# Two-layer hybrid DiT block: the first layer's middle modulation tiles by TensorE in column groups, and the stacking pattern loaded from DRAM

## The chip, the cores and the metric

The kernel runs on one core of one Trainium2 chip. The metric is the device time of one execution in microseconds. Engines are named as in the profile: PE (TensorE, matrix products), DVE (VectorE), ACT (ScalarE), POOL (GpSimd) and SP (SyncE, which issues most of the DMA transfers); ACT issues DMA transfers as well. Each engine runs its own instructions in order.

## The reference

The model has two layers. A modulation vector per layer comes from the conditioning c (and, for the 256 context tokens, from c_ctx):

```python
silu_c, silu_cc = silu(c), silu(c_ctx)
sh1, sc1, g1, sh2, sc2, g2 = split(silu_c @ ada_w[layer] + ada_b[layer], 6)        # 6 x 1024 columns
csh1, csc1, cg1, csh2, csc2, cg2 = split(silu_cc @ ada_w[layer] + ada_b[layer], 6)
a_l = rms_norm(h, norm1_g) * (1 + sc1) + sh1       # a_c likewise from hc
p = a @ w_in[layer]                                # columns of three head groups
d = diff_mixer(...)    # 4 heads, softmax(q1 k1) - lam * softmax(q2 k2), heads of 32
q = gqa_mixer(...)     # 6 query heads on 2 key heads of 64
n = gdn_mixer(...)     # gated DeltaNet: conv, l2 norm, chunks of 64, triangular solve, both directions
h = h + g1 * (concat(d, q, n) @ w_out)
h = h + g2 * swiglu(modulate(rms_norm(h, norm2_g), sh2, sc2))
```

There are 512 latent and 256 context tokens, and 1024 model columns. Only the latent stream is returned, after a last norm. The modulation has 48 column tiles of 128 per layer (6 x 1024), each for two conditionings. Tiles 0 to 15 (shift and scale of the first norm) are wanted first, tiles 16 to 23 (g1) after the output projection, 24 to 39 (shift and scale of the second norm) before the feed-forward part, 40 to 47 (g2) at the end.

## The kernel before

Activations lie with model columns on partitions. Projection products are split into three fp32r products: a weight block lands in a `raw` buffer, ACT rounds it to `whi`, DVE subtracts to get `wlo`, and PE multiplies ahi by whi, ahi by wlo and alo by whi. The ring `W` has three raw buffers of 128x1024 floats (512 KB); the `adaw` tiles of the modulation take their buffers from the same three. The weight loads that concern us (`w_t`, L160) and the adaw loads (L299) are issued from ACT's queue.

In layer 0 the start-up computes the norm and, in `ada_half` (L321 to L343), the first 16 modulation tiles: fp32 matmuls with the two conditionings (cT) as the weights and ada_w as the moving operand, 512 columns each, in two column groups. Then follow `gdn_inproj` (nine column tiles of the gated DeltaNet projection with their convolutions, PSUM tiles `gps`, evicted by ACT to `conv`), `zab` (six token tiles, PSUM tiles `tps`), and the groups dqk, kv and gq (six token tiles each). Between the groups, as `EARLY` (L41) orders it, stand the preparations ("0" to "5"), inversions ("v0" to "v2", the v0 of layer 0 on DVE, the other two on POOL) and posts of the DeltaNet part. After them the attention region begins, whose order `PLAN` (L37) gives; its start is `pick_setup` (L1080).

The 24 tiles 16 to 39 of layer 0 are made one per token tile of zab, dqk, kv and gq: `tok_group` calls `ada_next`, which loads a 512 KB tile of the transposed ada_w (128 output columns on partitions, 1024 inputs in a row) and, in `ada_row`, forms two row sums, one for each conditioning, against `cb`, that is silu(c) broadcast over the partitions by `ada_rows`. A row sum is one DVE operation with an accumulator (L183, output `junk`); for tiles 20 to 35 the second one is a product on POOL and an accumulating ACT copy. POOL adds the bias into `md`. The other layers' tiles and tiles 40 to 47 are made the same way, later.

`pick` is a 0/1 matrix of 128 x 4 x 128 by which PE stacks q and k heads (matmuls `stk`); `pick_setup` builds it with 64 DVE operations of 32x32 in each layer.

The order of instructions on each engine is set at build time by a scheduler that simulates the engines, from the order of the code and priorities; so a change of code in one place can move instructions of others.

Of the kernel before, what the change touches and what calls it, by code (L numbers as in the profile page):

```python
# [2 lines left out]

# [6 lines left out]
F32 = mybir.dt.float32  # L10
F32R = mybir.dt.float32r
I32 = mybir.dt.int32
AF = mybir.ActivationFunctionType
ALU = mybir.AluOpType
AX = mybir.AxisListType

D = 1024
KT = 8
# [21 lines left out]
INV_DVE = ((0,), (0, 2))  # L40
EARLY = ("0 1 2 5 4 v0 q v1 3 p0 p1 q q v2",  # L41
         "0 1 2 v0 5 v1 3 q p0 4 q p1 v2 q")
ADA_POOL = (tuple(range(20, 36, 1)), ())
LATF = (3, 4)
GORD = (("dqk", "kv", "gq"),) * 2
HORD = ((0, 2, 1, 3, 4),) * 2
# [52 lines left out]
class Net:  # L99
# [197 lines left out]
    def ada_row(self, R, w, l, ct, src, queue):  # L297

        queue.dma_start(out=w, in_=src)  # L299
        m = self.md[l][:, ct]  # L300
        j = R.tiny("junk", [128, 1024], mybir.dt.bfloat16)
        for ci in range(2):
            if ci == 1 and ct in ADA_POOL[l]:
                self.mul(w, w, self.cb[ci], self.g)
                self.act(w, w, AF.Copy, scale=0.5, accum_out=m[:, ci:ci + 1])
            else:
                self.stt(j, w, 0.5, self.cb[ci], ALU.mult, ALU.mult, accum_out=m[:, ci:ci + 1])
        self.add(m, m, self.adab[:, l, ct:ct + 1].to_broadcast([128, 2]), self.g)

    def ada_next(self):  # L310
# [10 lines left out]
    def ada_half(self, i, ws, pt):  # L321


        pd = self.big("adaps", i)
        ps, pd = pd[:, 0], (pd[:, 0], pd[:, 1])
        for kt, w in enumerate(ws):
            if i == 0:
                hi, lo = (self.R.tiny(n, [128, 1024], F32R, bufs=3) for n in ("adahi", "adalo"))
                for s in range(2):
                    j = slice(512 * s, 512 * s + 512)  # L330
                    self.cp(hi[:, j], w[:, j])
                    self.sub(lo[:, j], w[:, j], hi[:, j].bitcast(F32))
                for s in range(2):
                    j = slice(512 * s, 512 * s + 512)
                    self.mm(pd[s][0:4], self.cS[:, kt], hi[:, j], kt == 0, False)
                    self.mm(pd[s][0:4], self.cZ[:, kt], lo[:, j], False, kt == KT - 1)
                continue
            for s in range(2):
                self.lastrow = self.t.matmul(ps[64 * s:64 * s + 2], self.cT[:, kt], w[:, 512 * s:512 * s + 512], start=kt == 0, stop=kt == KT - 1).ins
        row = self.R.tiny("adar", [4, 2, 512], bufs=1)  # L340
        m = 4 if i == 0 else 2
        self.cp(row[0:m, 0], pd[0][0:m])
        self.v.tensor_copy(row[0:m, 1], pd[1][0:m] if i == 0 else ps[64:66])  # L343
        for s in range(2):
            for t in range(4):
                self.t.transpose(pt[:, 16 * s + 4 * t:16 * s + 4 * t + m], row[0:m, s, 128 * t:128 * t + 128], self.ident[0:m, 0:m])
        pv = pt[:, 0:32].rearrange("p (s t c) -> p s t c", s=2, c=4)
        md = self.md[0][:, 0:16].rearrange("p (s h t) c -> p s h t c", s=2, h=2)[:, :, i]
        b = self.adab[:, 0, 0:16].rearrange("p (s h t) -> p s h t", s=2, h=2)[:, :, i]
        self.add(md, pv[:, :, :, 0:2], b.unsqueeze(3).to_broadcast([128, 2, 4, 2]))  # L350
        if i == 0:
            self.add(md, md, pv[:, :, :, 2:4])
        kts = slice(4 * i, 4 * i + 4)
        self.stt(self.A1[0][:, 0, kts], md[:, 1], 1.0, self.gains[:, 0, kts].unsqueeze(2).to_broadcast([128, 4, 2]), ALU.add, ALU.mult)

    def ada_scale(self, l, n):
        o = 8 if n == 0 else 32
# [131 lines left out]
    def gdn_inproj(self, l):  # L489
        self.tokm = [[None] * 3 for _ in range(3)]  # L490
        for kind in range(3):
            for gi in range(3):
                if kind == 0 and gi == 0 and l == DEPTH - 1:
                    continue
                self.tokm[kind][gi] = self.G.slot("tokm", tag="k")
        self.gunits = {}
        if l > 0:
            self.gfirst = {}
        lat, ctx = (CTX, LAT, 262), (0, CTX, 2)
        order = (3, 4, 5, 0, 1, 2, 6, 7, 8)  # L500
        banks = {}
        for half in ((0, 256), (256, 256)):
            for i, ct in enumerate(order[:HALF[l]]):
                if ct not in banks:
                    banks[ct] = (self.mm_bank if i < 2 else self.aux)("gps")
                self.gdn_mm(l, ct, *lat, banks[ct], [half])
        for ct in order[HALF[l]:max(len(self.gfirst), LATF[l])]:
            self.gdn_mm(l, ct, *lat)
        for ct in order:
            if ct not in order[:max(LATF[l], HALF[l], len(self.gfirst))]:  # L510
                self.gdn_mm(l, ct, *lat)
            if ct > 2 or l < DEPTH - 1:
                self.gdn_mm(l, ct, *ctx)
            self.gdn_ct(l, *divmod(ct, 3))

    def tok_group(self, l, name, ncols, tiles, cols=None):
# [5 lines left out]
        for tt in tiles:  # L522
            lo_c, hi_c = cols(tt) if cols else (0, ncols)
            n = hi_c - lo_c
            ps = self.mm_bank("tps")
            for kt in range(KT):
# [4 lines left out]
                self.mm(ps[:, lo_c:hi_c], ah, wh, kt == 0, False)  # L531
                self.mm(ps[:, lo_c:hi_c], ah, wl, False, False)
                self.mm(ps[:, lo_c:hi_c], al, wh, False, kt == KT - 1)
            self.ada_next()
            yield tt, ps

    goff = {"zab": 0, "dqk": 8 * 408, "kv": 8 * 920, "gq": 8 * 1432}
# [542 lines left out]
    def pick_setup(self):  # L1080

        self.pick = self.R.tiny("pick", [128, 4, 128], F32R)
        for r in range(4):
            rows = slice(32 * r, 32 * r + 32)
            for j, at in enumerate(((0, 1), (2, 3), (0, 2), (1, 3))):
                for b in range(4):
                    self.v.tensor_scalar(out=self.pick[rows, j, 32 * b:32 * b + 32], in0=self.ident[rows, rows], scalar1=float(b in at), scalar2=None, op0=ALU.mult)

    def parts_of(self, t0):

# [370 lines left out]
    def build(self):  # L1461
# [7 lines left out]
        for l in range(DEPTH):  # L1469
# [2 lines left out]
            self.G = self.region("gdn%d" % l, sb, SLOT, k=12)  # L1472
            self.GP = self.P1 = self.region("prep%d" % l, sb, SLOT, s=P1S[l])
            self.R = self.region("proj%d" % l, sa, 512, s=PROJS[l])
            self.gdn_inproj(l)
            self.wprio, self.wafter = WPRIO[l], None
            if l == 0:
                self.ada_todo = [(0, ct) for ct in range(16, 40)]
                self.ada_rows(self.R)
            self.zab(l)  # L1480
            self.gdn_begin(l)
            proj = self.attn_proj(l)
# [31 lines left out]
            for kt in range(KT):  # L1514
                x = self.N.slot("h", tag="h")
# [13 lines left out]
            for b, R in self.ffn(l, whole, parts):  # L1529
                if last:  # L1530
                    for kt in range(KT):
                        x = self.hs(kt, *b[:2])
# [26 lines left out]
def shape_consts():  # L1559
    f = np.float32  # L1560
    i = np.arange(128)
    same = (i[:, None] // 64) == (i[None, :] // 64)
    l, j = i[:, None], i[None, :]
# [13 lines left out]
    def rope(rot):  # L1577
# [6 lines left out]
        t = np.stack([cc, ssn], 1).reshape(4, 128, 2, rot)  # L1584
        return np.ascontiguousarray(t.transpose(1, 0, 2, 3))

    return {"ident": np.eye(128, dtype=f), "masks": masks.reshape(128, 768), "mloc": mloc,
            "negm": np.concatenate([negm.reshape(128, 128), masks[:, 2:4].reshape(128, 256)], 1), "blk2": blk2,
            "rope_d": rope(32), "rope_g": rope(64)}

# [1 line left out]
def layout(inp):  # L1592
# [8 lines left out]
    aw = a["ada_w"]  # L1601
    o["ada_t"] = aw.transpose(0, 2, 1).reshape(96, 128, D)
    o["ada_q"] = aw[0, :, :2 * D].reshape(KT, 128, 2, 2, 512).transpose(3, 0, 1, 2, 4).reshape(2, KT, 128, D)
    o["adab"] = a["ada_b"].reshape(DEPTH, 48, 128).transpose(2, 0, 1)
    g = np.concatenate([a["norm1_g"], a["norm2_g"], a["final_norm_g"][None]], 0)
    o["gains"] = g.reshape(5, KT, 128).transpose(2, 0, 1)
    w = a["w_in"]
# [40 lines left out]
```

## Time and profile before

| | us |
|---|---|
| median of 3 runs | 2253.53 (2251.14 to 2255.30) |
| profiled execution | 2248.59 |
| span of the profiled execution, first to last instruction | 2246.8 |
| mean granted clock of PE in it | 0.923 |
| busy in the span: PE, DVE, ACT, POOL | 2019.5, 1466.3, 866.6, 562.8 |

The time of the profiled execution and its span differ by 1.8 us, which lies before the first and after the last instruction. Busy time of an engine is the time in which it had an instruction in work; the rest is waiting, and the view of lines says what ended it. In the trace, times are microseconds from the start of the span; PE is the matmuls and PEld the loads of weights, which may overlap them. "gps<-ahi,whi" means that gps is written from ahi and whi. A bracket behind a row of the timeline is the idle time of that engine before the row, and what ended it.

### The profile page before, as it was taken

The numbers are of one execution on the slowest core, as the hardware profiler recorded it, in microseconds if no ns is written. First come the engines' busy times: TensorE is split into PE (matmuls) and PEld (weight loads), VectorE is DVE, ScalarE is ACT, GpSimd is POOL, SyncE is SP. The second block draws the span as 40 slices with busy tenths as digits, with TensorE's granted clock in tenths as the row PEclk, the third lists the DMA queues.
The fourth block names the chain that finished last, engine by engine and source line by source line (L and its number), as shares of the span: only waits on it lengthen the run. The fifth ranks groups of instructions, "written<-read, shape, count | busy, mean of one in ns | idle before, by whom it ended". The sixth has DMA issues, their size and how long they took to land. (4 is left out here: it accounts for less than half of the span.)

```text
span 2246.8 us, 37406 instructions
## 1 busy us (share of the span) xinstructions
PE 2019.5 (90%) x14588; PEld 1680.6 (75%) x14588; DVE 1466.3 (65%) x2756; ACT 866.6 (39%) x1738; POOL 562.8 (25%) x835
## 2 busy tenths in 40 slices
PE   7997865889889999999999989985799899999997
PEld 3885654666668888888888888764567688888887
DVE  6888896857653766746667467678767745434444
ACT  5443322665662421212121344322466644222223
POOL 2137687522003300000000240347213022000002
PEclk9998975799889999999999989996589999999999
DMA  8145543221033334433334321443312153322331
GB/s 303 53 148 151 166 142 96 47 63 48 25 137 123 100 114 140 142 102 127 128 108 146 107 71 54 131 122 93 68 31 65 38 189 100 97 79 95 104 104 61
DMA packets 167601, 237.01 MB, mean 105 GB/s; under 512 B 75329, under 2 KB 109249, under 8 KB 167425
## 3 DMA queue, kind: packets, MB, share of 16 engines
q10 hardware_dynamic: 46160, 144.92, 19.8%
q1 hardware_dynamic: 121264, 89.70, 13.3%
q8 instruction: 115, 1.88, 0.3%
q14 instruction: 62, 0.50, 0.1%
HBM read 198.53 MB, written 36.04 MB: 104 GB/s over the span
## 5 line engine op out<-in xcount | busy, mean ns | idle before, releaser
L189 ACT ACTIVATE whi<-raw 128x1024 fp32r<-128x1024 f32 (+4 forms) x246 | 220.8, 912 | 470.2 <-PE dps L192 200.6
L165 DVE TENSOR_TENSOR wlo<-raw,whi 128x1024 fp32r<-128x1024 f32 (+4 forms) x236 | 249.2, 1069 | 197.0 <-ACT whi L189 196.2
L192 PE MATMUL gu<-ahi,wlo 128*128 128x512 f32 x672 | 262.5, 391 | 1.6 <-DVE wlo L165 1.6
L192 PE MATMUL gu<-ahi,whi 128*128 128x512 f32 x672 | 262.2, 391 | 0.0
L183 DVE SCALAR_TENSOR_TENSOR junk<-adaw,cb 128x1024 bf16<-128x1024 f32 x144 | 179.7, 1248 | 40.9 <-DMA adaw<-ada_t 39.9
L192 PE MATMUL dps<-acth,whi 128*128 128x512 f32 (+1 forms) x560 | 184.3, 344 | 0.6 <-ACT acth L189 0.4
L192 PE MATMUL dps<-acth,wlo 128*128 128x512 f32 (+1 forms) x560 | 183.9, 344 | 0.0
L192 PE MATMUL gu<-alo,whi 128*128 128x512 f32 x672 | 167.0, 390 | 0.0
L165 POOL TENSOR_TENSOR md<-md,adab 128x2 f32<-128x2 f32 x80 | 44.2, 555 | 451.4 <-DVE junk L183 449.0
L192 PE MATMUL tps<-whi,ahi 128*128 128x512 f32 (+4 forms) x368 | 138.0, 378 | 15.0 <-ACT gk L189 12.5
L183 DVE SCALAR_TENSOR_TENSOR h<-dps,md,h 128x512 f32<-128x512 f32 (+1 forms) x128 | 80.4, 632 | 104.8 <-PE dps L192 104.7
L1140 DVE TENSOR_REDUCE nm<-S 128x1 f32<-128x768 f32 (+1 forms) x140 | 117.3, 844 | 47.9 <-PE S L192 46.9
L192 PEld LDWEIGHTS gu<-ahi,wlo 128*128 128x128 f32 x672 | 126.3, 188 | 28.1 <-DVE wlo L165 2.0
L192 PEld LDWEIGHTS gu<-alo,whi 128*128 128x128 f32 x672 | 126.1, 188 | 26.7
L192 PEld LDWEIGHTS gu<-ahi,whi 128*128 128x128 f32 x672 | 126.3, 188 | 25.7
L165 POOL TENSOR_TENSOR sqc<-sqc 128x256 f32<-128x256 f32 x35 | 34.4, 983 | 435.7 <-ACT sqc L186 435.2
L192 PE MATMUL tps<-wlo,ahi 128*128 128x512 f32 (+4 forms) x368 | 139.0, 378 | 2.5 <-DVE wlo L165 2.5
L192 PE MATMUL tps<-whi,alo 128*128 128x512 f32 (+4 forms) x368 | 137.4, 374 | 0.0
L186 ACT ACTIVATE P<-S,nm 128x768 f32<-128x768 f32 (+1 forms) x140 | 114.3, 817 | 45.3 <-DVE nm L1140 33.0
L192 PE MATMUL dps<-actl,whi 128*128 128x512 f32 (+1 forms) x560 | 122.9, 344 | 0.0
L192 PEld LDWEIGHTS dps<-acth,whi 128*128 128x128 f32 x560 | 105.2, 188 | 15.2 <-ACT acth L189 0.6
L192 PEld LDWEIGHTS dps<-acth,wlo 128*128 128x128 f32 x560 | 105.2, 188 | 14.5
(311 smaller groups left out, 4846.9 us busy)
## 6 DMA issues: line engine op xcount, KB each, us to landing
raw<-w_u ACTq DMA_DIRECT2D x88, 512.0 KB
adaw<-ada_t ACTq DMA_DIRECT2D x80, 512.0 KB
raw<-w_o ACTq DMA_DIRECT2D x24, 512.0 KB
raw<-w_d ACTq DMA_DIRECT2D x44, 256.0 KB
raw<-w_d ACTq DMA_DIRECT2D x32, 320.0 KB
adaq<-ada_q SPq DMA_DIRECT2D x16, 512.0 KB
raw<-w_t ACTq DMA_DIRECT2D x16, 512.0 KB
h<-h SPq DMA_DIRECT2D x16, 384.0 KB
```

The source lines that it names most:

```text
L165: (eng or self.v).tensor_tensor(out=out, in0=a, in1=b, op=op)
L183: self.v.scalar_tensor_tensor(out=out, in0=a, scalar=sc, in1=b, op0=op0, op1=op1, **k)
L186: self.s.activation(out=out, in_=in_, func=func, **k)
L189: self.s.activation(out=out, in_=in_, func=AF.Copy, **k)
L192: self.t.matmul(out, lhsT, rhs, start=start, stop=stop)
L1140: self.v.tensor_reduce(out=nm, in_=pin, axis=AX.XY if nk == 768 else AX.X, op=ALU.max, negate=True)
```

## The change

Layer 0's tiles 16 to 39 are no longer made by row sums. A generator `ada_cols` makes them on PE, 24 steps in all: for each of three blocks of 1024 output columns (j) and each of eight blocks of 128 inputs (kt), it loads a 128x1024 block of ada_w (inputs on partitions) from a new DRAM input `ada_p`, and multiplies it by cW, which holds the two conditionings in the first 2 of 32 columns and zeros in the others. Each of the four 256-column quarters goes to its own column group of 32, so one step is four fp32 matmuls. After eight steps ACT evicts 128x256, PE transposes it in two halves, and DVE adds the bias into md. Two steps are taken in each round of the last loop of `gdn_inproj` (18), and one per token tile of zab (6). `ada_rows` is not called for layer 0, and the variant of `ada_row` on POOL is gone.

`pick` comes as an input: one DMA of 256 KB into a slot of the tag that dq and dk use, and one copy on ACT, in each layer.

```diff
             if ct > 2 or l < DEPTH - 1:
                 self.gdn_mm(l, ct, *ctx)
+            for _ in range(2):
+                next(self.ada_step)
             self.gdn_ct(l, *divmod(ct, 3))
...
-            self.ada_next()
+            next(self.ada_step)
             yield tt, ps
...
+    def ada_cols(self):
+        c = self.R.tiny("cW", [128, KT, 32])
+        self.g.memset(c, 0.0)
+        self.g.tensor_copy(c[:, :, 0:2], self.cT)
+        big = self.big("adaps", 1)
+        for j in range(3):
+            ps = big[:, j // 2, 256 * (j % 2):256 * (j % 2) + 256]
+            for kt in range(KT):
+                w = self.W.slot("adaw", F32, "raw")
+                self.nc.scalar.dma_start(out=w, in_=self.A["ada_p"][j, kt])
+                for q in range(4):
+                    self.t.matmul(ps[32 * q:32 * q + 32], c[:, kt], w[:, 256 * q:256 * q + 256], start=kt == 0, stop=kt == KT - 1)
+                yield
+            row = self.R.tiny("adar", [128, 256])
+            self.cp(row, ps)
+            pt = big[:, 1, 256:512]
+            for b in range(2):
+                self.tr(pt[:, 128 * b:128 * b + 128], row[:, 128 * b:128 * b + 128])
+            cts = slice(16 + 8 * j, 24 + 8 * j)
+            self.add(self.md[0][:, cts]..., pt..., self.adab[:, 0, cts]...)
+        while True:
+            yield
...
     def pick_setup(self):
         self.pick = self.R.tiny("pick", [128, 4, 128], F32R)
-        for r in range(4):
-            rows = slice(32 * r, 32 * r + 32)
-            for j, at in enumerate(((0, 1), (2, 3), (0, 2), (1, 3))):
-                for b in range(4):
-                    self.v.tensor_scalar(out=self.pick[rows, j, 32 * b:32 * b + 32], in0=self.ident[rows, rows], scalar1=float(b in at), scalar2=None, op0=ALU.mult)
+        raw = self.slot("pickraw", tag="d")[:, :512]
+        self.dma(raw, self.A["pick"])
+        self.cp(self.pick.rearrange("p a b -> p (a b)"), raw)
...
+            self.ada_step = self.ada_cols() if l == 0 else itertools.repeat(None)
             self.gdn_inproj(l)
             self.wprio, self.wafter = WPRIO[l], None
-            if l == 0:
-                self.ada_todo = [(0, ct) for ct in range(16, 40)]
-                self.ada_rows(self.R)
```

On PE, in the first column tiles of the in-projection (gps are its PSUM tiles, ahi, alo, whi and wlo the split operands), these rows followed each other before:

```order
L192 MATMUL gps_466<-alo_308,whi_346 128x512
L192 MATMUL gps_466<-alo_309,whi_346 128x512
L192 MATMUL gps_427<-ahi_294,whi_340 128x512
L192 MATMUL gps_427<-ahi_294,wlo_341 128x512
L192 MATMUL gps_440<-ahi_294,whi_342 128x512
```

Now, in the same place:

```order
L192 MATMUL gps_466<-alo_308,whi_346 128x512
L192 MATMUL gps_466<-alo_309,whi_346 128x512
L365 MATMUL adaps_671<-adaw_672,cW_668 32x256 x4
L365 MATMUL adaps_671<-adaw_678,cW_668 32x256 x4
L365 MATMUL adaps_671<-adaw_730,cW_668 32x256 x4
L192 MATMUL gps_427<-ahi_294,whi_340 128x512
L192 MATMUL gps_427<-ahi_294,wlo_341 128x512
```

Three of the 24 steps stand together between gps matmuls; the others come singly or in twos and threes, in some 18 places of the in-projection and of zab, and the rest of PE's order there is as before but for small shifts.

On ACT, in the in-projection (whi is the split of a raw block, conv the eviction of a gps, w_t the first weights of zab; a DMA row is the issue of a load), before:

```order
L160 DMA raw_1248<-w_t 128x816
L189 ACTIVATE whi_1155<-raw_1154 128x1024
L189 ACTIVATE tokm_570<-ctr_684 128x2x128
L189 ACTIVATE conv_832<-gps_836 128x512
L189 ACTIVATE conv_832<-gps_862 128x256
L186 ACTIVATE conv_603<-cacc_714 128x772
L160 DMA raw_1254<-w_t 128x816
L160 DMA raw_1260<-w_t 128x816
```

Now, four column tiles later, where gps_1175 and gps_1201 belong to the last column tile but one and gps_1269 and gps_1295 to the last:

```order
L189 ACTIVATE conv_1171<-gps_1201 128x256
L363 DMA adaw_1332<-ada_p 128x1024
L189 ACTIVATE tokm_571<-ctr_1153 128x2x128
L189 ACTIVATE tokm_572<-ctr_1157 128x2x128
L160 DMA raw_1360<-w_t 128x816
L189 ACTIVATE adar_1321<-adaps_671 128x256
L189 ACTIVATE whi_1361<-raw_1360 128x816
L186 ACTIVATE conv_1171<-cacc_1239 128x772
L189 ACTIVATE tokm_573<-ctr_1161 128x2x128
L160 DMA raw_1366<-w_t 128x816
L189 ACTIVATE conv_1265<-gps_1269 128x512
L189 ACTIVATE whi_1367<-raw_1366 128x816
```

The loads of zab's weights moved behind adaw loads, from the middle of the in-projection to its last two column tiles.

On DVE, at the start of layer 0's attention region (gk are keys after rotation, qT the transposed queries that are stacked), before:

```order
L165 TENSOR_TENSOR gk_3245<-rt_3302,rt2_3304 128x384
L165 TENSOR_TENSOR gk_3283<-rt_3310,rt2_3312 128x384
L1087 TENSOR_SCALAR pick_3505<-ident_92 32x32 x64
L165 TENSOR_TENSOR qT_3575<-exp_3576,qT_3574 128x256
L165 TENSOR_TENSOR qT_3575<-exp_3581,qT_3574 128x512
```

Now:

```order
L797 STREAM_TRANSPOSE ZT_2583<-Z_2577 128x768
L165 TENSOR_TENSOR rt_3295<-gk_3244,ropeq_2709 128x384
L165 TENSOR_TENSOR rt_3303<-gk_3276,ropeq_2709 128x384
L165 TENSOR_TENSOR gk_3244<-rt_3295,rt2_3297 128x384
L165 TENSOR_TENSOR gk_3276<-rt_3303,rt2_3305 128x384
L165 TENSOR_TENSOR qT_3507<-exp_3508,qT_3506 128x256
L165 TENSOR_TENSOR qT_3507<-exp_3513,qT_3506 128x512
```

The 64 operations are gone, and qT follows gk; a transposition of the inversion (ZT) has moved ahead of the last rotations.

## Rows read from the trace of the kernel before

**Rows 1.** The head of the page: span, and busy time of the engines.
```profile
span 2246.8 us, 37406 instructions
PE 2019.5 (90%) x14588; PEld 1680.6 (75%) x14588; DVE 1466.3 (65%) x2756; ACT 866.6 (39%) x1738; POOL 562.8 (25%) x835
```

**Rows 2.** Windows: stretch, length, busy us of each engine, clock, DMA share, GB/s.
```profile
37.00:156.00 119.00, 113.92 (x648) 100.07 (x647) 102.13 (x119) 57.10 (x111) 37.00 (x53) 0.99 0.33 105
156.00:352.00 196.00, 144.65 (x1034) 117.90 (x1032) 171.68 (x324) 64.94 (x125) 140.05 (x181) 0.83 0.49 148
190.00:230.00 40.00, 29.59 (x165) 22.62 (x165) 26.63 (x34) 11.42 (x20) 35.06 (x62) 0.91 0.53 154
270.00:310.00 40.00, 24.45 (x137) 18.60 (x135) 37.88 (x75) 8.83 (x16) 30.85 (x31) 0.71 0.52 173
310.00:352.00 42.00, 31.36 (x438) 29.89 (x438) 36.43 (x77) 13.69 (x31) 34.17 (x54) 0.70 0.36 99
352.00:374.00 22.00, 5.35 (x58) 4.41 (x58) 20.36 (x70) 1.85 (x5) 17.93 (x33) 0.50 0.37 101
1570.00:1584.00 14.00, 3.86 (x29) 2.63 (x29) 13.62 (x74) 0.60 (x1) 6.91 (x9) 0.50 0.64 153
```

**Rows 3.** Lines of DVE, 156 to 310: busy, mean ns, idle before.
```profile
L183 DVE SCALAR_TENSOR_TENSOR junk<-adaw,cb 128x1024 bf16<-128x1024 f32 x22 | 28.5, 1297 | 7.9 <-DMA adaw<-ada_t 7.9
```

**Rows 4.** Lines of POOL in the same stretch.
```profile
L165 POOL TENSOR_TENSOR adaw<-adaw,cb 128x1024 f32<-128x1024 f32 x14 | 38.9, 2782 | 31.4 <-DVE junk L183 31.4
L165 POOL TENSOR_TENSOR md<-md,adab 128x2 f32<-128x2 f32 x18 | 7.3, 411 | 2.4 <-ACT adaw L186 2.4
```

**Rows 5.** Windows of the tile junk alone: DVE busy, clock, DMA.
```profile
270.00:310.00 40.00, 12.17 (x20) 0.71 0.52 173
```

**Rows 6.** The tile adaw: ns least, median, most; two belong to layer 0.
```profile
L183 DVE SCALAR_TENSOR_TENSOR cb<-adaw,cb x4: 1212/1214/1226, 84.8 to 723.3; 128x1024 f32<-128x1024 f32 x4
```

**Rows 7.** Timeline of PE from 33 us: start, us, what.
```profile
33.69 3.60 PE L339 MATMUL adaps<-adaq,cT 128*2 128x512 f32 x16
...
39.64 0.39 PE L192 MATMUL gps<-ahi,whi 128*128 128x512 f32 x1
39.87 0.39 PE L192 MATMUL gps<-ahi,wlo 128*128 128x512 f32 x1
40.18 1.03 PE L339 MATMUL adaps<-adaq,cT 128*2 128x512 f32 x4
41.14 0.50 PE L192 MATMUL gps<-ahi,whi 128*128 128x512 f32 x1
41.48 0.40 PE L192 MATMUL gps<-ahi,wlo 128*128 128x512 f32 x1
```

**Rows 8.** Timeline of the weight loads in the same place.
```profile
40.18 0.09 PEld L339 LDWEIGHTS adaps<-adaq,cT 128*2 128x2 f32 x4 [0.35 <-issue]
```

**Rows 9.** Timeline, 89 to 127 us: loads, splits and their use.
```profile
89.56 2.46 ACTq L160 DMA_DIRECT2D raw<-w_t  x2
...
98.80 0.89 ACT L189 ACTIVATE whi<-raw 128x816 fp32r<-128x816 f32 x1 [0.52 <-PE gps L192]
...
118.73 0.33 ACTq L299 DMA_DIRECT2D adaw<-ada_t  x1
...
122.20 1.23 DVE L183 SCALAR_TENSOR_TENSOR junk<-adaw,cb 128x1024 bf16<-128x1024 f32 x1 [0.23 <-DMA adaw<-ada_t]
...
126.48 0.43 PE L192 MATMUL tps<-whi,ahi 128*128 128x408 f32 x1
```

**Rows 10.** Timeline of layer 0 at the stacking pattern.
```profile
353.27 18.81 DVE L1087 TENSOR_SCALAR pick<-ident 32x32 fp32r<-32x32 f32 x64 [2.03 <-DMA dgq<-gk]
...
357.17 0.60 ACT L189 ACTIVATE qT<-exp 128x512 fp32r<-128x512 f32 x1 [0.47 <-PE exp L195]
...
372.59 1.82 PE L192 MATMUL stk<-qT,pick 32*128 32x256 f32 x4 [13.05 <-DVE qT L165]
```

**Rows 11.** Timeline of layer 1 at the stacking pattern.
```profile
1584.24 1.22 PE L192 MATMUL stk<-qT,pick 32*128 32x512 f32 x3 [3.79 <-DVE qT L165]
```

More of the change, by code (lines that the diff above doesn't have):

```diff
@@ L1 @@
+import itertools
 import math
@@ L42 @@
          "0 1 2 v0 5 v1 3 q p0 4 q p1 v2 q")
-ADA_POOL = (tuple(range(20, 36, 1)), ())
 LATF = (3, 4)
@@ L302, in ada_row @@
         for ci in range(2):
[L303 to L307, printed above, removed]
+            self.stt(j, w, 0.5, self.cb[ci], ALU.mult, ALU.mult, accum_out=m[:, ci:ci + 1])
         self.add(m, m, self.adab[:, l, ct:ct + 1].to_broadcast([128, 2]), self.g)
@@ L354, in ada_half @@
         self.stt(self.A1[0][:, 0, kts], md[:, 1], 1.0, self.gains[:, 0, kts].unsqueeze(2).to_broadcast([128, 4, 2]), ALU.add, ALU.mult)
+    def ada_cols(self):
[17 more added lines that the diff above has]
+            cts = slice(16 + 8 * j, 24 + 8 * j)
+            self.add(self.md[0][:, cts].rearrange("p (q b) c -> p q b c", b=2), pt.rearrange("p (b q x) -> p q b x", b=2, q=4)[:, :, :, 0:2],
+                     self.adab[:, 0, cts].rearrange("p (q b) -> p q b", b=2).unsqueeze(3).to_broadcast([128, 4, 2, 2]))
+        while True:
+            yield
     def ada_scale(self, l, n):
@@ L1585, in rope @@
         return np.ascontiguousarray(t.transpose(1, 0, 2, 3))
-    return {"ident": np.eye(128, dtype=f), "masks": masks.reshape(128, 768), "mloc": mloc,
+    pick = np.zeros((4, 32, 4, 4, 32), f)
+    for j, at in enumerate(((0, 1), (2, 3), (0, 2), (1, 3))):
+        for b in at:
+            pick[:, :, j, b] = np.eye(32, dtype=f)
+    return {"ident": np.eye(128, dtype=f), "pick": pick.reshape(128, 512), "masks": masks.reshape(128, 768), "mloc": mloc,
             "negm": np.concatenate([negm.reshape(128, 128), masks[:, 2:4].reshape(128, 256)], 1), "blk2": blk2,
@@ L1603, in layout @@
     o["ada_q"] = aw[0, :, :2 * D].reshape(KT, 128, 2, 2, 512).transpose(3, 0, 1, 2, 4).reshape(2, KT, 128, D)
+    o["ada_p"] = aw[0, :, 2 * D:5 * D].reshape(KT, 128, 3, D).transpose(2, 0, 1, 3)
     o["adab"] = a["ada_b"].reshape(DEPTH, 48, 128).transpose(2, 0, 1)
```

## The prediction

> **What bounds the kernel now.** I read the head of the page first: PE is busy for 90% of a span of 2246.8 us, DVE for 65%, ACT for 39%, POOL for 25% [rows 1]. That average hides the place of the change, so I cut the first 400 us into stages with the view of windows [rows 2]. Two regimes are to be seen there. From 37 to 156 us (the gated DeltaNet in-projection and zab) PE is busy for 113.9 of 119 us: it is the bound, and DVE, with 102.1, has some room. From 156 to 352 us (the dqk, kv and gq groups, with the preparations and inversions between them) PE falls to 144.7 of 196, while DVE holds 171.7 and at 270 to 310 even 37.88 of 40. POOL takes over once, at 190 to 230, with 35.06 of 40. So a microsecond of DVE or POOL saved before 156 is worth little; saved after it, it can be worth itself; and a microsecond of PE added before 156 costs itself. From 352 to 374 PE works 5.35 of 22 us.
>
> Next I grouped the lines of DVE and POOL in 156 to 310 us, where row sums stand [rows 3 to 5], and what ada_rows costs [rows 6]; then I looked at the nearest relative of the new matmuls, ada_half [rows 7, 8], at the loads that share the raw ring [rows 9], and at the two places of the stacking pattern [rows 10, 11].
>
> **The change, part by part.** The sum is made against the profiled execution, 2248.59 us (1.8 us outside its span). It lies 4.9 us below the median of the runs, 2253.53, and I add these 4.9 at the end.
>
> *New matmuls, +16.* There are 24 steps, each of four fp32 matmuls that write 32 partitions by 256 columns. The relative has two column groups (row starts 0 and 64) of 512 columns, also on all 128 rows: sixteen records in 3.60 us, four of them to a step, so 0.90 us a step [rows 7]. A lone step stands between gps matmuls that start at 39.87, 41.14 and 41.48; undisturbed, such starts lie 0.23 apart (39.64, 39.87). The step thus took 1.61 - 0.46 = 1.15 us, of which 0.25 is its edges. The new step streams half as many columns in each group. If four groups run side by side as two do, it is 0.45; if the array gives no more than the two groups gave, 0.90; if the groups run one after another, 1.80. No row shows four groups on the same rows; I take 0.45, since two groups are seen to overlap and nothing in the rows sets two apart from four. The order gathers the 24 steps into some 18 visits: 24 x 0.45 + 18 x 0.25 = 15.3, and six transposes at about 0.15 (an estimate from the 0.23 of a four times wider matmul, with room for the switch) make it 16.2. The ends are 24 x 0.90 + 5.4 = 27 and 24 x 1.80 + 5.4 = 49 upward, and 24 x 0.45 = 11 downward. All of it stands where PE is the bound, so nothing hides it.
>
> Four LDWEIGHTS of the relative lie inside 0.09 us, though all use the same 128 rows [rows 8]. The Trainium skill, "TensorE: Matmul & The Clock Gate", Part 3, says that a weight load overlaps running matmuls only where the row group differs; that would leave the eight loads of each new step bare, at no more than 0.09 each 0.7 us a step and 17 in all, and the forecast would be about 2243. The trace disagrees, and I don't take it.
>
> *Waits for the raw ring, +9.* The 24 loads of 512 KB use three raw buffers that the in-projection's weights also use, and their issues stand in ACT's queue, ahead of evictions for which PE's banks wait. One such stall is in the trace: the issue of two w_t loads took 2.46 us at 89.56 [rows 9]. The larger item is zab's weights. Before, the first of four w_t units is split at 98.80 and zab's first matmul starts at 126.48, 28 us later [rows 9]. After, the first unit is loaded between the evictions of the last two column tiles, and as two adaw tiles hold two of the buffers, units two and three go through one buffer in turn. One turn is a load of 3.5 (issue 118.73, use 122.20 [rows 9]), a split on ACT and one on DVE of about 1 each: 5.5 us. Three turns last 16.5, and PE has the rest of the last column tile and the first parts of two token tiles to set against them, about 10. So 6 to 7 us of stall there, and 2 for ACT's queue: 9. Ends: 0 if the ring runs ahead, 20 if each of twelve loads of the in-projection stops PE for 1 us more.
>
> *Row sums gone, -30.* In 156 to 310 us 22 sums of 1297 ns on DVE, and 7.9 us in which DVE waits for their loads, make 36.4 us [rows 3]. POOL loses 14 products of 2782 ns, 38.9 us, and 7.3 of additions into md [rows 4]; ACT loses the sums of these products. What I count is the DVE part, since DVE is the bound of that stretch; POOL's counts at 190 to 230 only. The row sums before 156 lie under a full PE and give nothing. Upper end: 36.4 and POOL's 7.3, 44. Lower end: 12, the junk work of 270 to 310 alone [rows 5], where PE has only 24.45 and DVE 37.88 of 40 [rows 2]. After the change PE's 144.7, DVE's 171.7 - 28.5 = 143 and POOL's inversion (34.17 of 42 at 310 to 352) are close together, so not all of it can come through. I take 30.
>
> *Stacking pattern of layer 0, -13.* DVE spends 18.81 us in 64 small operations from 353.27; ACT's half of qT starts at 357.17, but DVE's half waits behind them, and PE waits 13.05 us for it, to 372.59 [rows 10]. After, the pattern is a 256 KB load on SP ahead of dq's and one ACT copy of about 0.6. PE's start falls to some 358.5: 14, less 1 for the load put before dq's. What is late next is POOL, 17.93 of 22 busy there [rows 2]; if its inversion holds the scans, 4 are left. Ends 15 and 4.
>
> *Stacking pattern of layer 1, -7.* There the 64 operations lie between inversion steps on DVE, which is busy for 13.62 of 14 us [rows 2]; PE has done one stacking matmul before and then waits 3.79 us for DVE's qT, to 1584.24 [rows 11]. With those inversion steps in the 13.62, I set the 64 operations at about 10 us of DVE (an estimate; layer 0's price of 18.81 would not fit in). 1 goes to the load and 2 to the inversion steps that still precede. Ends 0, if the inversion sets that place anyway, and 11.
>
> *ada_rows gone, -2.* Two DVE operations of 1214 ns in the in-projection [rows 6], where DVE has most but not all of the time. Ends 0 and 2.4. The memset and copy of cW, three evictions and three small additions I cost at nothing: POOL has 37.0 of 119 us busy there, ACT 57.1, and the last addition falls where DVE is relieved. Were that cover gone, they would cost 3.
>
> Sum: 16 + 9 - 30 - 13 - 7 - 2 = -27. 2248.6 - 27 = 2221.6 by the profile; with the 4.9 for the median it is 2226.
>
> **The rivals.**
>
> *A, the relief is hidden.* Without the row sums, 156 to 352 is paced by PE, the preparation chains and POOL's inversion in their order, and only 12 come back; the patterns give 8 and 4. For it: POOL's 34.17 of 42 and PE's 31.36 in the last of these stretches. Against: DVE's 37.88 and 36.43 [rows 2]. 2253.5 + 16 + 9 - 12 - 8 - 4 - 1 = 2253, no change.
>
> *B, the groups don't overlap.* A step costs 1.80: 49 instead of 16. 2226 + 33 = 2259, slower; the gain is used up from (27 + 10.8) / 24 = 1.6 us a step. Against it stands the relative, whose two groups overlap.
>
> *C, the in-projection starves.* PE takes each adaw tile at a fixed row; where its load is late, all gps matmuls behind it stop. 18 visits late by 2.5 us each are 45 instead of 9: 2226 + 36 = 2262, slower. It decides from (27 + 9) / 18 = 2 us a visit. For it: the 2.46 us stall, and three buffers shared by two streams. Against: the DMA share is only 0.33 there [rows 2], and a load takes 3.5.
>
> *D, everything counts.* Relief 44, no stalls, patterns at 15 and 10: 2253.5 + 16 + 1 - 44 - 15 - 10 - 2 = 2199.
>
> *E, POOL's inversion takes the place of layer 0's pattern:* 4 instead of 13, 2235, inside the forecast's own range.
>
> **How the numbers follow.** A measurement of this kernel can tell about 0.2%, 4.5 us, so faster means below 2249 and slower above 2258. The forecast with its own bounds (E among them) gets 0.58, D 0.18, A 0.12, B 0.05, C 0.07. Half of A counts as same, a quarter to each side; of the forecast's cases 0.01 lie at same. Faster: 0.58 - 0.01 + 0.18 + 0.03 = 0.78; slower: 0.05 + 0.07 + 0.03 = 0.15; same 0.07. The forecast's own range is 2208 to 2246; toward D I go to 2196, toward A to 2251.
>
> **What would show it.** L365's matmuls at 0.45 to 0.5 us a step, and PE's busy time up to the end of zab 11 to 16 higher; zab's first matmuls waiting for splits for about 6 us; the end of the gq groups (now 352) near 347, that is 25 later from the in-projection and 30 earlier from the relief; qT within 2 us of its transposes in both layers. Against me: steps of 0.9 or more (pairs at best, B at 1.8), PE waiting for adaw loads in the in-projection (C), or a middle stage as long as before with DVE idle in it (A).

## The result, and the profile after

The changed kernel takes 2220.97 us (median of 4 runs, 2220.56 to 2223.04), against 2252.34 before (4 runs, 2245.08 to 2255.30). The ratio of the runs is 0.9874, 95% interval 0.9846 to 0.9901, which makes some 28 us; the medians lie 31 apart, the profiled executions 27.9. The forecast was 2226, faster. Its sum came out right, but by luck: terms of it were off by up to 20 us, and a stretch that it left out made up for them.

The head of the page after, for [rows 1]:

```profile
span 2218.9 us, 37524 instructions
PE 2038.1 (92%) x14786; PEld 1688.2 (76%) x14786; DVE 1371.7 (62%) x2565; ACT 850.0 (38%) x1709; POOL 494.0 (22%) x797
```

DVE is busy for 95 us less and PE for 19 more, and the span is 27.9 shorter. Where the time went is seen when both executions are cut at the same instructions instead of the same times: the first gps, the first zab matmul, the first dqk matmul, layer 0's first exp, its first stk and the first gu of the feed-forward part. The windows of before by these cuts (stretch, length, PE, PEld, DVE, ACT, POOL, clock, DMA share, GB/s), for [rows 2]:

```profile
37.22:126.48 89.26, 84.68 (x487) 71.58 (x485) 77.02 (x92) 43.13 (x80) 21.93 (x42) 0.98 0.29 90
126.48:156.13 29.65, 29.15 (x165) 28.62 (x164) 25.02 (x28) 13.88 (x31) 15.07 (x12) 1.00 0.47 147
156.13:355.60 199.47, 144.53 (x1034) 117.77 (x1033) 173.88 (x330) 64.81 (x125) 143.65 (x189) 0.83 0.50 150
355.60:372.59 16.99, 3.94 (x55) 3.42 (x55) 16.92 (x62) 1.47 (x3) 14.33 (x25) 0.50 0.31 82
372.59:733.26 360.67, 317.12 (x3161) 244.09 (x3161) 217.87 (x523) 200.86 (x493) 91.11 (x124) 0.86 0.26 78
```

The same cuts after:

```profile
37.66:137.53 99.87, 97.31 (x628) 76.67 (x627) 71.49 (x81) 42.65 (x83) 23.64 (x42) 0.98 0.43 140
137.53:174.13 36.60, 34.43 (x220) 28.33 (x218) 13.05 (x17) 10.98 (x26) 5.04 (x5) 1.00 0.56 179
174.13:323.61 149.48, 133.88 (x1039) 110.45 (x1035) 116.83 (x281) 50.25 (x98) 89.16 (x162) 0.92 0.46 141
323.61:327.48 3.87, 3.87 (x54) 3.42 (x55) 1.12 (x2) 1.47 (x3) 3.87 (x9) 0.50 1.22 299
327.48:705.73 378.25, 324.38 (x3163) 248.78 (x3162) 225.55 (x523) 202.05 (x493) 97.87 (x136) 0.84 0.25 75
```

Up to the first dqk matmul 18 us are added (10.6 and 7.0 in the windows, 0.4 before them). The middle stage, from the first dqk matmul to the first exp, is 50.0 shorter, and PE is now busy for 133.9 of its 149.5 us: it has become the bound there. The pattern (first exp to first stk) gives 13.1. Then something shows that no step of the forecast had: layer 0's attention region, here the stretch from the first stk to the first gu, whose code the change leaves as it was, takes 17.6 us longer, with the same matmuls (3161 and 3163 in the two windows). From the first gu on both need the same (1513.5 and 1513.2). 18.0 - 50.0 - 13.1 + 17.6 - 0.4 = -27.9.

The new steps on PE, for [rows 7], three together, with their weight loads, then one alone in zab:

```profile
51.97 1.50 PE L365 MATMUL adaps<-adaw,cW 128*32 128x256 f32 x24
51.97 0.59 PEld L365 LDWEIGHTS adaps<-adaw,cW 128*32 128x32 f32 x16 [0.35 <-issue]
52.77 0.22 PEld L365 LDWEIGHTS adaps<-adaw,cW 128*32 128x32 f32 x8 [0.21 <-DMA adaw<-ada_p]
53.40 0.50 PE L192 MATMUL gps<-ahi,whi 128*128 128x512 f32 x1
...
168.04 0.34 PE L192 MATMUL tps<-whi,alo 128*128 128x408 f32 x1
168.32 0.64 PE L365 MATMUL adaps<-adaw,cW 128*32 128x256 f32 x8
168.89 0.45 PE L192 MATMUL tps<-whi,ahi 128*128 128x408 f32 x1
169.18 0.35 PE L192 MATMUL tps<-wlo,ahi 128*128 128x408 f32 x1
```

A step is eight records, two for each of its four fp32 matmuls. Three steps from 51.97 to 53.40 are 0.48 each, near the 0.45 of the sum. The lone one cost 169.18 - 168.04 less two spacings of 0.187, 0.77 us, so its edges are 0.3 rather than 0.25.

zab's beginning, for [rows 9], with its waits in the brackets:

```profile
139.39 0.72 PE L192 MATMUL tps<-whi,ahi 128*128 128x408 f32 x2 [0.49 <-ACT whi L189]
...
145.07 0.63 PE L192 MATMUL tps<-whi,ahi 128*128 128x408 f32 x2 [0.75 <-ACT whi L189]
146.11 0.46 PE L192 MATMUL tps<-wlo,ahi 128*128 128x408 f32 x1 [0.41 <-DVE wlo L165]
...
148.76 0.64 PE L192 MATMUL tps<-whi,ahi 128*128 128x408 f32 x2 [0.52 <-ACT whi L189]
```

These are all the waits for zab's late weights: 2.2 us, not 6 to 7.

What ended PE's waits in the middle stage before (us in total, times, longest), the three lines that end on POOL:

```profile
PE qet L195 <- POOL qeg L165: 11.2, 2, 8.3
PE seg L192 <- POOL Gm L165: 10.4, 3, 6.7
PE wps L817 <- POOL Tg L165: 6.5, 1, 6.5
```

And after:

```profile
PE wps L841 <- POOL Z L787: 0.5, 1, 0.5
PE wps L841 <- POOL Yg L165: 0.5, 1, 0.5
```

So 28.1 of the 54.9 us in which PE was idle there ended on POOL, and 1.0 of 15.6 after. The next rows, of the kernel before, show the tie between POOL and DVE: a product of a row sum on POOL that waited for DVE's sum, an operation of the inversion on DVE beside it, and the same operation with POOL idle.

```profile
275.73 3.51 POOL L165 TENSOR_TENSOR adaw<-adaw,cb 128x1024 f32<-128x1024 f32 x1 [7.33 <-DVE junk L183]
276.90 2.60 DVE L165 TENSOR_TENSOR Tg<-Yg 96x234 f32<-96x234 f32 x1
...
262.83 0.39 DVE L165 TENSOR_TENSOR Tg<-Yg 96x234 f32<-96x234 f32 x1
```

The operation beside the product ends behind the product's end. Next to twelve of the fourteen products of this stage an operation of DVE is stretched in this way; the releasers in the lines above are those that came last by the profile.

The pattern of layer 0 after, for [rows 10]:

```profile
318.54 0.37 SPq L156 DMA_DIRECT2D pickraw<-pick  x1
319.00 0.63 SPq L156 DMA_DIRECT2D dq<-dqk  x1
...
321.33 0.63 ACT L189 ACTIVATE pick<-pickraw 128x512 fp32r<-128x512 f32 x1 [3.41 <-DMA pickraw<-pick]
...
323.61 1.54 PE L195 MATMUL exp<-ident,dq 128*128 128x128 f32 x6 [3.81 <-DMA dq<-dqk]
...
325.82 0.69 DVE L165 TENSOR_TENSOR qT<-exp,qT 128x512 fp32r<-128x512 f32 x1 [0.64 <-ACT qT L189]
...
327.48 1.64 PE L192 MATMUL stk<-qT,pick 32*128 32x256 f32 x4
```

DVE's half of qT follows ACT's at once; the last wait of PE before its stack is now the one for dq. In layer 1, for [rows 11]:

```profile
1543.22 1.11 PE L195 MATMUL exp<-ident,dq 128*128 128x128 f32 x4 [5.86 <-DMA dq<-dqk]
...
1548.03 0.68 DVE L165 TENSOR_TENSOR qT<-exp,qT 128x512 fp32r<-128x512 f32 x1
...
1549.46 1.22 PE L192 MATMUL stk<-qT,pick 32*128 32x512 f32 x3
```

From exp to the three matmuls behind DVE's qT it is 6.2 us instead of 12.6 (1571.63 to 1584.24), yet nothing of it is left at the first gu of layer 1.

### The profile page after: what moved, and what is told of

Same layout as the page of the kernel before. It is cut to its first block, busy times and chain, and to the rows that moved or that the text cites. A ratio compares the mean times of both kernels' runs of the same rounds, so it can differ in the third digit from the quotient of the medians.

```text
span 2218.9 us, 37524 instructions
## 1 busy us (share of the span) xinstructions
PE 2038.1 (92%) x14786; PEld 1688.2 (76%) x14786; DVE 1371.7 (62%) x2565; ACT 850.0 (38%) x1709; POOL 494.0 (22%) x797
## 3 DMA queue, kind: packets, MB, share of 16 engines
q1 hardware_dynamic: 121264, 89.18, 13.2%
## 5 line engine op out<-in xcount | busy, mean ns | idle before, releaser
L183 DVE SCALAR_TENSOR_TENSOR junk<-adaw,cb 128x1024 bf16<-128x1024 f32 x112 | 136.9, 1222 | 37.2 <-DMA adaw<-ada_t 36.3
L165 POOL TENSOR_TENSOR md<-md,adab 128x2 f32<-128x2 f32 x56 | 33.0, 588 | 434.9 <-DVE junk L183 434.9
```

The lines of the kernel that those rows point to most:

```text
L165: (eng or self.v).tensor_tensor(out=out, in0=a, in1=b, op=op)
L183: self.v.scalar_tensor_tensor(out=out, in0=a, scalar=sc, in1=b, op0=op0, op1=op1, **k)
```

## The experiments

Two theories were open at first. Theory 1: the parts add up as in my sum. Theory 2: a lead with which the attention region is reached is given back in it. Kernels with only a part of the change are to tell them apart. All times within a kernel come from one execution, the profiled one; it is the longest of the runs of ada_only, twice and no_middle, and the shortest of those of step_prio0, pick_l0 and one_per_ct.

**pick_only.** The edit to the kernel before:

```diff
-        for r in range(4):
...
-                        self.v.tensor_scalar(out=self.pick[rows, j, 32 * b:32 * b + 32], in0=self.ident[rows, rows], ...)
+        raw = self.slot("pickraw", tag="d")[:, :512]
+        self.dma(raw, self.A["pick"])
+        self.cp(self.pick.rearrange("p a b -> p (a b)"), raw)
```

Expected: 

> The kernel before with the stacking pattern loaded from DRAM in both layers, and nothing else of the change. Theory 1, my sum, in which the parts add up: 13 us in layer 0 and 7 in layer 1, so 20 us less than before (about 2232). Theory 2, read from the two traces, in which a lead at the pattern is given back later in the same attention region: the first stk matmul of layer 0 about 13 us earlier, but the first gu matmul and the end within 4 us of before, a total of 0 to -4 us.

Measured: 2236.65 against 2249.93, ratio 0.9952 (0.9936 to 0.9967), some 11 us: between the two. Its start of the attention region:

```profile
352.95 0.33 SPq L156 DMA_DIRECT2D pickraw<-pick  x1
353.38 0.62 SPq L156 DMA_DIRECT2D dq<-dqk  x1
...
358.25 1.54 PE L195 MATMUL exp<-ident,dq 128*128 128x128 f32 x6 [6.88 <-DMA dq<-dqk]
...
362.12 1.64 PE L192 MATMUL stk<-qT,pick 32*128 32x256 f32 x4
```

exp starts 2.7 us later than before (358.25 against 355.60): 0.8 were there before the pattern, and it waits 1.9 longer for dq, whose load now follows the pattern's; so stk gains 10.5, not 14. Of these, 2.5 go at the next stk, which waits 3.6 us for DVE's qs instead of 1.0. Matmul by matmul the lead is then 8.0 through nearly the whole region, 9.7 in the feed-forward part and 13.3 at the end. PE's order of matmuls up to layer 1's attention is that of before. So theory 2 is wrong for this part: behind these 2.5 us nothing is given back where the order stays.

**ada_only.** The edit puts the 64 DVE operations of each layer back into the changed kernel. Expected: 

> The changed kernel with the stacking pattern built again by 64 operations on DVE in each layer. Theory 1: without the 20 us of the pattern, 7 to 8 us less than before (about 2244). Theory 2: the row sums are worth more than the 30 of my sum, and nearly all of the 28 us stays: about 2224 to 2228, with the first exp of layer 0 some 32 us earlier than before.

Measured: 2228.82 us, ratio 0.9901 (0.9885 to 0.9917), 22 us; theory 1's 8 are refuted. So the row sums taken off DVE and POOL give most of the gain. The first stk comes 33.9 us earlier than before, the first gu only 17.1: half of this lead goes in the attention region, which takes 377.4 us.

**no_middle.** The edit:

```diff
-            self.ada_step = self.ada_cols() if l == 0 else itertools.repeat(None)
+            self.ada_step = itertools.repeat(None)
+            if l == 0:
+                self.v.tensor_copy(self.md[0][:, 16:40], self.adab[:, 0, 16:40]...)
```

Expected: 

> The changed kernel without any computation of layer 0's 24 middle tiles: no loads, no matmuls, no row sums, the tiles are the bias alone (that part of the output is left out). It prices the work that is put on PE against none. Theory 1: 25 us less than the changed kernel (16 of matmuls and 9 of waits for the ring), about 2196. Theory 2: up to the end of zab it is 18 us earlier than the changed kernel, as the traces differ there, but a lead is partly given back in the attention region, so 8 to 15 us less, about 2207 to 2213.

This kernel leaves out the middle modulation. Measured: 2185.11, ratio 0.9717 (0.9701 to 0.9732), some 35 us under the changed kernel, more than either theory. In the traces 16 of 30 us are there at the first gu of layer 0; the other 14 come in layer 1, where the edit changes no line (more on this below). Its first dqk matmul is at 156.4 and that of the changed kernel at 174.1, so the steps and their loads cost 17.7 us up to there.

**one_group.** The edit:

```diff
+                    o = q if kt == 0 else 0
-                    self.t.matmul(ps[32 * q:32 * q + 32], ..., start=kt == 0, stop=kt == KT - 1)
+                    self.t.matmul(ps[32 * o:32 * o + 32], ..., start=kt == 0, stop=q == 3 and kt == KT - 1 if o == 0 else True)
```

Expected: 

> The changed kernel with 21 of the 24 steps sending their four matmuls to one column group instead of four (only the first step of each block uses four; the sums of three quarters are wrong). If the four groups overlap, a step here costs about 1.8 us instead of 0.43 to 0.64: PE's busy time in the in-projection and zab up by 25 to 29 us and the time by as much, less what is given back (about 2236 to 2250). If the groups do not overlap (rival B), nothing changes.

Measured: 2235.31, ratio 0.9936 (0.992 to 0.9951), 14 us over the changed kernel. PE is busy for 25 us more up to the first dqk matmul, as expected. Two places of its timeline on PE:

```profile
182.79 1.91 PE L366 MATMUL adaps<-adaw,cW 128*32 128x256 f32 x8
...
195.81 1.91 PE L366 MATMUL adaps<-adaw,cW 128*32 128x256 f32 x8
```

A lone step's eight records take 1.91 us in one group and 0.64 in four, so the groups do run side by side. The first dqk matmul is 23.5 us later than in the changed kernel (21 x 1.27 = 27 at most). Rival B is refuted.

In the kernels without row sums PE's order in layer 0's attention region is another one than before. Count successive matmuls of one kind as one row: of the 1342 rows of the region before, 1194 keep their sequence in the changed kernel, while every row of pick_only does. Theory O: the region's length hangs on the order that the scheduler happens to find. Rival G: a region that is reached early gives back its lead whatever the order.

**twice.** The edit:

```diff
+                    for r in range(2):
-                    self.t.matmul(..., start=kt == 0, stop=kt == KT - 1)
+                        self.t.matmul(..., start=kt == 0 and r == 0, stop=kt == KT - 1 and r == 1)
...
-            self.cp(row, ps)
+            self.act(row, ps, AF.Copy, scale=0.5)
```

Expected: 

> The changed kernel with each matmul of the 24 steps issued twice, and the eviction halved. The double work costs PE 24 x 0.43 = 10 us in the in-projection and zab. But PE's order in layer 0's attention region (first stk to first gu) is row for row that of the kernel before here, while the changed kernel has another one and takes 378 us for it against 361. Theory O (the order makes the region longer): the region takes 360 to 363 us, and in spite of the double work the total falls by 5 to 9 us against the changed kernel, to about 2213. Rival G (a region that starts earlier gives back its lead whatever the order, for instance by the clock): the region stays at 374 to 380 and the total rises by 8 to 10 us, to about 2230.

The premise was mistaken: in the trace only 1221 of the 1342 rows keep before's sequence. Measured: 2218.66, ratio 0.9854 (0.9835 to 0.9872), between the two forecasts. The double work made stk 12.1 us later, and the region took 368.4, 9.9 less than in the changed kernel. So it says little between O and G: the region is shorter, it also starts later and has a third order.

**one_per_ct.** The edit:

```diff
-            for _ in range(2):
+            for _ in range(1):
                 next(self.ada_step)
```

Expected: 

> The changed kernel with one step of the 24 in each round of the in-projection instead of two, so that nine of them move from there to the dqk and kv groups. PE's order in layer 0's attention region is again that of the kernel before. Theory O: the region takes 360 to 363 us, the first zab matmul comes 4 to 6 us earlier than in the changed kernel, and the total falls by 15 to 22 us against it, to 2199 to 2206. Rival G: the region stays at 374 to 380, and the total falls by 0 to 6.

The same mistake, and a larger one: some 390 matmuls of the DeltaNet part that stood before the first stk now stand behind it (3550 records in the region, 3163 in the changed kernel), so the region's length can't be set beside the others. Measured: 2197.25, ratio 0.9767 (0.9741 to 0.9793), some 24 us under the changed kernel and the best of the versions that compute everything. Its first zab matmul is 5.5 us earlier, as expected, and stk 8.5; the region took 374.0, not 360 to 363. 12.7 of 25.0 us in the traces are there at the first gu, a cut that holds the same work on both sides; the other 12 come in layer 1.

**tok_only.** All steps move to the token groups (the loop above goes, with one more call after the last group). Expected: 

> The changed kernel with all 24 steps at the token tiles of zab, dqk, kv and gq, one at each, as the row sums were, none in the in-projection. PE's order in layer 0's attention region is neither that of the kernel before nor that of the changed one. If waits for the raw ring in the in-projection are most of its 11 us, the first zab matmul is back at 127 us (before: 126.5). Theory O leaves the length of the region open (355 to 385); the sum says the 24 steps cost the same 10 to 16 us of PE later, so the total is 2205 to 2230.

Measured: 2231.23, ratio 0.991 (0.9892 to 0.9927), just over the expected range. The first zab matmul is at 129.1, but POOL's second inversion ends at 431 us instead of 372, and the region, which holds 3708 records here, takes 424.4.

**pick_l0.** DVE builds the pattern in layer 1 only. Expected: 

> The changed kernel with layer 1's stacking pattern built again by 64 operations on DVE. My sum: 7 us more than the changed kernel (2228). By the kernel with the pattern alone, whose lead grew from 9.7 us at the end of layer 0 to 13.3 at the end: 3 to 4 us more (2225).

Measured: 2219.51, ratio 0.986 (0.9842 to 0.9879), not slower than the changed kernel's 0.9874 (0.9846 to 0.9901). The load in layer 1 brought nothing that can be measured here. The run shows one thing more: PE's order in layer 0's region is that of the changed kernel, here and in ada_only (1360 of 1360 and 1356 of 1358 rows). The changed kernel, pick_l0 and ada_only reach the region at 327.5, 323.8 and 338.7 us and take 378.3, 377.8 and 377.4 for it: with one order the length stays, though the start moves by 15 us. pick_only with before's order does the same (362.0 against 360.7, 10.5 us earlier).

**step_prio0 and step_prio1000.** The edit is one number, tried on the changed kernel:

```diff
-SPRIO = (300, 1000)
+SPRIO = (0, 1000)        # and (1000, 1000)
```

Expected: 

> The changed kernel with the scheduler's priority of the DeltaNet steps of layer 0 at 0 instead of 300. PE's order up to layer 0's attention region is that of the changed kernel row for row; in the region (first stk to first gu) 737 of 993 rows keep their sequence. Theory O (the length of the region hangs on the order that the scheduler finds there): the region, 378 us in the changed kernel, changes by 6 us or more either way, and the total with it. Rival G (the region gives back a lead with which it is reached, whatever the order): 374 to 381 us, and a total within 4 us of the changed kernel's 2221.

> The same with the priority at 1000: 924 of 993 rows of the region keep their sequence, all before it does. Theory O: a change of the region by some us, smaller than that of the kernel with priority 0, and the total with it. Rival G: 374 to 381 us, total within 4 us of 2221.

Measured: 2209.49, ratio 0.9818 (0.9782 to 0.9853), and 2208.65, ratio 0.9821 (0.9783 to 0.9859), each some 12 us under the changed kernel. All eight runs (2201.79 to 2216.85) lie under its four, but the intervals just touch, and the trace of step_prio0 is of its quickest run. The region's window in the two, in that order:

```profile
325.11:690.20 365.09, 312.60 (x3163) 239.56 (x3161) 222.35 (x521) 200.41 (x493) 96.83 (x136) 0.88 0.26 78
```

```profile
326.42:695.42 369.00, 312.66 (x3163) 240.18 (x3161) 222.46 (x521) 201.51 (x493) 97.73 (x136) 0.87 0.26 77
```

Reached within 2.4 us of the same time, with the same order before it and the same matmuls, the region is 13.2 and 9.3 us shorter than after the change. PE's busy time in it falls by 11.8 and 11.7 us, at a higher clock; in the second its idle time grows by 2.5. Rival G alone is refuted, theory O holds here.

**one_per_ct_p0 and one_per_ct_p1000.** The same edit on one_per_ct. Expected: 

> One step in each round of the in-projection, with the priority of layer 0's DeltaNet steps at 0. PE's order up to layer 0's attention region is that of the kernel with one step a round (2197 us); in the region 960 of 1179 rows keep their sequence. Theory O: the region, 374 us there, changes by 6 us or more either way, total 2180 to 2215. Rival G: 370 to 378 us, total within 5 us of 2197.

> The same with the priority at 1000; in the region 1124 of 1179 rows keep their sequence. Theory O: a change of the region by some us, and if both gains add as they did apart (24 for one step a round, 12 for the priority), about 2185. Rival G: total within 5 us of 2197.

Measured: 2220.78, ratio 0.9888 (0.9863 to 0.9912), and 2208.49, ratio 0.9832 (0.9811 to 0.9853): both slower than one_per_ct, and the gains do not add. With priority 0 the region takes 383.8 us, 9.8 more than in one_per_ct with the same matmuls, where on the changed kernel it took 13 less; with 1000 it keeps its length, 374.1, though PE is busy for 6.5 us less in it. The order matters by about 10 us, but neither value is the better one in itself.

All the regions together (us; "PE" is the number of PE's records in the region; "low" is the time at the lower clock level, granted clock 0.50, in it; "rest" runs from the first gu to the end). Regions with 3160 to 3163 records hold the same work, and so do the three with 3550 or 3551; others are not to be compared:

| kernel | first stk | region | PE | PE busy in it | low | rest |
|---|---|---|---|---|---|---|
| before | 372.6 | 360.7 | 3161 | 317.1 | 98 | 1513.5 |
| pick_only | 362.1 | 362.0 | 3163 | 314.8 | 93 | 1509.6 |
| one_group | 350.0 | 372.7 | 3163 | 323.5 | 117 | 1512.3 |
| twice | 339.6 | 368.4 | 3162 | 325.2 | 117 | 1512.9 |
| ada_only | 338.7 | 377.4 | 3160 | 325.9 | 123 | 1514.4 |
| changed | 327.5 | 378.3 | 3163 | 324.4 | 120 | 1513.2 |
| step_prio1000 | 326.4 | 369.0 | 3163 | 312.7 | 96 | 1512.7 |
| step_prio0 | 325.1 | 365.1 | 3163 | 312.6 | 86 | 1509.7 |
| pick_l0 | 323.8 | 377.8 | 3162 | 323.3 | 118 | 1512.0 |
| no_middle | 311.3 | 378.5 | 3211 | 328.0 | 116 | 1499.0 |
| one_per_ct_p0 | 321.0 | 383.8 | 3551 | 332.9 | 125 | 1513.8 |
| one_per_ct | 319.0 | 374.0 | 3550 | 324.2 | 105 | 1500.9 |
| one_per_ct_p1000 | 318.3 | 374.1 | 3550 | 317.8 | 85 | 1513.4 |
| tok_only | 295.4 | 424.4 | 3708 | 348.2 | 131 | 1508.6 |

In the last column one_per_ct and no_middle stand apart: they lie 8 to 15 us under all the others. They share an order of layer 1's groups (1245 of 1249 rows, counted as above) that none of the others has, one_per_ct_p0 and _p1000 included. So half of one_per_ct's gain over the changed kernel goes with an order in layer 1, not with the place of the steps. That nothing else differs there was not tried.

## Why the prediction was right, step by step

- *New matmuls, +16:* right in size. PE's busy time up to the end of zab rose by 12.6 and 5.3, 17.9 us; the step of 0.48 and the edges of 0.3 make 24 x 0.48 + 18 x 0.3 = 17. Four groups overlap as I took them to (one_group). The rule on weight loads in the Trainium skill, "TensorE: Matmul & The Clock Gate", Part 3, which I set aside, does not hold in this trace: the loads from 51.97 to 52.56 and from 52.77 to 52.99 lie under matmuls that run without a gap from 51.97 to 53.47, all on the same 128 rows.
- *Waits for the raw ring, +9:* this step failed. PE's idle time up to the first dqk matmul did not rise (4.58 and 0.50 us before, 2.56 and 2.17 after). Zab's weights came late as I read from the order, but by 2.2 us. PE had more to set against the loads than I counted: between the units stand steps (143.24 to 144.31, 149.76 to 150.40) and the transposes ctr of the in-projection. Rival C falls with it.
- *Row sums gone, -30:* this step failed, in size and in mechanism; the measured 50 us lie beyond my upper end of 44. I counted DVE's sums and loads, 36.4, as the bound's time, gave POOL's products a value at 190 to 230 only, and took PE's 144.7 busy us as fixed. But half of PE's idle time ended on POOL (28.1 of 54.9 us), whose products stood in its queue ahead of qeg, Gm and Tg and waited for DVE's sums themselves. And the products held DVE up: its busy time fell by 57.1 us (173.88 to 116.83), while the sums and a few pick operations are only 33. The rest is less time for work that stayed: 279 operations that both windows hold in equal numbers took 159.3 us before and 129.9 after, added up one by one. That the products are the cause is read from the traces; no run takes them alone away. In all PE's idle time fell by 39 us (54.9 to 15.6). The other 11 are PE's own busy time, 144.5 to 133.9 for the same matmuls, as the clock rose from 0.83 to 0.92: a stage that waits less also ran faster, and this term was missing. Rival A is refuted, and of D only this part came.
- *Pattern of layer 0, -13:* 13.1 by the windows, but 8 to 10 in what is left of it behind the first stacks (pick_only). The load put ahead of dq's cost 1.9 instead of 1. Rival E did not come: POOL's second inversion ended 44 us after the first stk, as before.
- *Pattern of layer 1, -7:* mis-sized; between nothing (pick_l0) and 3.6 (the lead in pick_only from 9.7 to 13.3). DVE's qT does come 6 us sooner behind exp, but from exp to the first gu of layer 1 it is 318.9 us after and 318.4 before: the attention behind it gives that back.
- *ada_rows, -2:* can't be told from the rest of the in-projection.
- *Not in the sum, +17.6:* the attention region. I took the order behind the pattern as given, since only a few rows of the pattern's place were compared; the scheduler had laid out the whole region anew. The priorities show that its order alone moves it by 9 to 13 us, on the changed kernel through PE's busy time and the clock. Here is the longest stretch at the lower clock that begins in the region of the changed kernel:

```profile
496.00:502.00 6.00, 4.59 (x44) 3.68 (x44) 5.94 (x31) 1.08 (x2) 0.00 (x0) 0.70 0.16 44
502.00:508.00 6.00, 6.00 (x44) 4.16 (x43) 2.98 (x7) 1.19 (x2) 0.00 (x0) 0.50 0.00 1
508.00:514.00 6.00, 6.00 (x38) 3.72 (x37) 4.18 (x9) 4.08 (x9) 1.15 (x2) 0.50 0.12 36
514.00:520.00 6.00, 4.68 (x16) 3.11 (x14) 5.87 (x16) 3.87 (x9) 0.81 (x1) 0.50 0.11 33
```

The clock falls at 498.4, after PE has waited three times for DVE since 496 (1.4 us together; DVE is busy for 5.94 of 6 there), and stays at the lower level for 27 us, though by the profile PE is then busy without a gap for 12 of them. The low time of the region went from 98 to 120 us, and PE's busy time from 317.1 to 324.4; the other 10 us are idle time, for which no single wait stands out.

So 2226 was luck, from errors that cancel: 25 for the new work where 18 were due, 30 for the relief where 50 were, 20 for the patterns where 13 came in layer 0 and nothing clear in layer 1, and nothing for a region that took 17.6. Of the signs that I named, the step's time came, and PE's busy time rose by 2 more than the 11 to 16; zab's wait was a third of mine. The gq groups did not end 5 us earlier but 34 (their last tps at 298.6 instead of 332.6), and qT in layer 1 came 4.8 us behind its transposes, not 2. What stays open is whether a region that is reached 45 us earlier would take 361 us in the old order: with either order the length held where the start moved by 10 to 15, and no kernel here had the old order and the early start.

## What to carry to other kernels

Ask which engine ends the waits of the one that matters, not only which engine is busiest: here DVE was the fullest, but POOL ended half of PE's waits, and each held up the other. Relief can be worth more than the time of the work taken away, since PE's own matmuls ran faster once the waits were gone; read the clock of the stage beside its busy times. When a scheduler orders the program, compare the order of all that follows and not only of the place edited: here an order that nobody chose cost some 10 us, and one number in a priority gave them back, while on a near relative the same number cost as much. Check that two cuts hold the same work before their lengths are compared. And price a part alone in a kernel whose order stays: pick_only gave a lead that can be read off matmul by matmul, the others did not.

## What the runs showed of the hardware that was not expected

Four column groups of 32 on the same 128 rows take 0.64 us for a lone step that takes 1.91 in one group, a factor of 3. An operation of DVE that runs for 0.39 us alone took 2.60 beside a product of POOL, and ended just behind it; this holds beside twelve of fourteen products, and why it spares the others was not tried. And the lower clock level can last: 27 us in one piece, with PE busy by the profile for 6.00 of 6 us twice in it.
